# Stage one of a decoder layer in a written order, with constant products on TensorE, and the second pair's key sums two hooks later

## The chip, the cores and the metric

The kernel runs on one core of one Trainium2 chip. The metric is the device time of one execution in microseconds, the median over the runs. Engines are named as in the profile: PE (TensorE, products), DVE (VectorE), ACT (ScalarE), POOL (GpSimd) and SP (SyncE, which here only issues transfers).

## The reference

One decoder layer (DEPTH 1) on x of 1024 tokens by 1024 features. In the cut below `A`, `B` and `C` are the three head groups; the change touches the first product and the keys of group C.

```python
def rmsnorm(x, g):
    xf = x.astype(jnp.float32)
    y = xf * lax.rsqrt(jnp.mean(xf * xf, axis=-1, keepdims=True) + NORM_EPS)
    return (y * g.astype(jnp.float32)).astype(x.dtype)
...
    z = rmsnorm(h, norm_mix_g[l]) @ w_in[l]
    a_q, a_f, a_i, a_g, b_q, b_k, b_v, c_in = jnp.split(z, splits, axis=-1)
    o_a = hgrn2_mix(a_q, a_f, a_i, a_g, lbs[l], hgrn_gnorm_g[l])
    o_b = dilated_window_mix(b_q, b_k, b_v)
    o_c, v_first = rwkv7_mix(c_in, ...)
    h = h + jnp.concatenate([o_a, o_b, o_c], axis=-1) @ w_out[l]
    h = h + conv_glu_ffn(rmsnorm(h, norm_ffn_g[l]), ffn_up[l], ffn_conv_w[l], ffn_conv_b[l], ffn_down[l])
    gate = jax.nn.sigmoid(rmsnorm(h, norm_ple_g[l]) @ ple_gate[l])
    h = h + gate * (p[l] @ ple_proj[l])
return rmsnorm(h, final_norm_g)
...
# in rwkv7_mix: the keys are scaled to length one per head
    kk = heads(k * k_k)
    kk = kk / jnp.maximum(jnp.linalg.norm(kk, axis=-1, keepdims=True), 1e-12)
```

## The kernel before

The work lies with features on the 128 partitions and tokens along a row. x comes as eight blocks of 128 features by 1024 tokens, in two halves of 512 tokens (`hf` 0 and 1). A weight block (`w_in[j]`) has 128 output features by 1024 inputs.

Products are made from split operands: ACT casts a high part (`whi`, `xh`), DVE or POOL subtracts it for the low part (`wlo`, `xl`), and `mm3` issues three products of 128 by 512, hi by hi (L127), hi by lo (L129) and lo by hi (L131). A block of weights takes 8 steps `k` of three products for each half. Two low parts are made per block; `split_w` gives them to POOL and DVE in turn.

Stage one is `mix_norm`. It loads x, the first three weight blocks and the parameters `par`, and makes the products of blocks 0, 1 and 2 with x times the norm's weight `g`, but without the norm's factor per token. That factor is made beside it: ACT squares x (`ssq`), DVE adds the eight squares up (`acc`), PE sums them over the partitions (`factor_sums`, L164, out `ps_ss`), DVE and POOL make the reciprocal root (`rst`), and PE spreads it over the partitions (`factor`, L174), from where ACT copies it to `rstd`. The products' results (`dp`) are multiplied by `rstd` later.

Then `rwkv` works on two pairs of heads (p = 0, 1). `rwkv_prep` projects k, r and v (`mix_in`), each 8 steps with both halves, so 48 products. Functions hung in as hooks are called after a step of such a projection. The keys' path is: `key_norm` (ACT squares k into `kksq`), `key_sums` (PE sums them, L530, out `kks`; DVE and POOL make `kr`), `removal_keys` (PE spreads `kr`, L182, out `kkb`; DVE makes `kkn`, a, `ar` and `bhat`). From `bhat` ACT and POOL make blocks `bb`, and PE the scores `sc` (L608).

What sets the order: instructions of one engine run in the order in which they stand in its program. Where nothing is written, a scheduler chooses it from what is ready by its own reckoning. Inside `tc.manual_schedule(engines=...)` the engines named keep the order of the code; `rwkv_prep` has that for PE. SP, ACT and POOL each issue transfers on a queue of their own. The transfers of stage one all stand on SP's queue, except the last columns of `par` on POOL's.

Of the kernel before, what the change touches and what calls it, by code (L numbers as in the profile page):

```python
# [10 lines left out]
F32 = mybir.dt.float32  # L11
F32R = mybir.dt.float32r
U8 = mybir.dt.uint8
AF = mybir.ActivationFunctionType
# [4 lines left out]
P = 128  # L19
T = 1024  # L20
HT = 512
ND = 8
# [57 lines left out]
class Trunk:  # L80
# [244 lines left out]
    def mix_norm(self):  # L325


        nc = self.nc
        X = self.xall()
        self.X = X  # L330
        self.R = self.keep.tile([P, T], F32, name="rstd")
        g = self.par[:, PC_MIX:PC_MIX + ND]
        halves = [slice(hf * HT, (hf + 1) * HT) for hf in (0, 1)]
        self.ps0 = ExitStack()
        ps0 = self.ps0.enter_context(self.pool("ps0", space=PSUM))
        with self.tc.tile_pool(name="st", bufs=1) as sp:
            dummy = sp.tile([P, 1], F32, name="dummy")
            nc.scalar.activation(dummy, self.ones, AF.Square)
            nc.sync.dma_start(self.par[:, :PC_LORA], self.a["par"][:, :PC_LORA])
            xs = [[sp.tile([P, 2, HT], F32, name=f"x{k}_{hf}") for k in range(4)] for hf in (0, 1)]  # L340
            xT = self.a["xT"].rearrange("(a two) p t -> a p two t", two=2)
            raws = {}
            for hf, sl in enumerate(halves):
                raws[hf] = self.wpool.tile([P, 1024], F32, tag="wraw", name=self.nm("wraw"), bufs=2)
                nc.sync.dma_start(raws[hf], self.a["w_in"][hf])
                for k in range(4):
                    nc.sync.dma_start(xs[hf][k], xT[k][:, :, sl])
                if hf == 0:
                    raws[2] = sp.tile([P, 1024], F32, name="wraw2")
                    nc.sync.dma_start(raws[2], self.a["w_in"][2])  # L350
            self.load_params()
            w = {j: self.split_w(raws[j]) for j in (0, 1)}
            self.early = {j: self.dps.tile([P, T], F32, tag="dp", name=self.nm("dp")) for j in (0, 1)}
            self.early[2] = ps0.tile([P, T], F32, name="dp2")
            def split(hf, k, acc):
                x = xs[hf][k // 2][:, k % 2, :]
                hi, lo = X[k][0][hf], X[k][1][hf]
                nc.scalar.activation(hi, x, AF.Copy, scale=g[:, k:k + 1])  # L358
                nc.vector.scalar_tensor_tensor(lo, x, g[:, k:k + 1], hi.bitcast(F32), ALU.mult, ALU.subtract)  # L359
                t = sp.tile([P, HT], F32, tag="ssq", name=self.nm("ssq"), bufs=4) if k else acc  # L360
                nc.scalar.activation(t, x, AF.Square)
                if k:
                    nc.vector.tensor_tensor(acc, acc, t, ALU.add)

            def first_two(hf, k):
                for j in (0, 1):
                    self.mm3({hf: self.early[j][:, halves[hf]]}, w[j](k), X[k], k == 0, k == ND - 1, (hf,))

            def factor_sums(acc):
                return self.rstd_sums(acc, 1.0 / 1024, EPS, ps0.tile([P, 4], F32, tag="n", name=self.nm("ps_ss"), bufs=2))  # L370

            def factor(hf, r):
                pb = self.rstd_spread(r, ps0.tile([P, HT], F32, tag="n", name=self.nm("ps_ss"), bufs=2))
                nc.scalar.copy(self.R[:, halves[hf]], pb)

            acc = [sp.tile([P, HT], F32, tag="sacc", name=self.nm("acc"), bufs=2) for _ in halves]
# [108 lines left out]
    def rwkv_prep(self, p, tp, lt, d, j):  # L485

        tc, nc, par = self.tc, self.nc, self.par
# [7 lines left out]
        def c3(t):  # L495
            return t.rearrange("p (c i) -> p c i", i=64)
# [25 lines left out]
        def key_norm():  # L522
            sq = tr("kksq")
            nc.scalar.activation(sq, d["k"], AF.Square, scale=col(PC_KK))
            d["kksq"] = sq
# [1104 lines left out]
```

## Time and profile before

| what | value |
|---|---|
| median of 3 runs | 1525.62 us (1524.99 to 1525.76) |
| profiled execution | 1523.62 us, span 1521.6 us |
| instructions | 20022 |
| mean granted TensorE clock | 0.986 |
| ACT busy, POOL busy | 634.1 us, 434.8 us |
| HBM read, written | 120.12 MB, 46.40 MB |

The span goes from the first to the last instruction of the profiled execution, and the execution's time is 2.0 us longer. In the rows of the profile, a line `L127 PE MATMUL dp<-xh,whi` is an instruction of line 127 on PE that writes `dp` from `xh` and `whi`; behind it stands how many are merged in the row, and in brackets how long the engine had been idle and what ended that. In a row of windows there stand, for each engine, its busy microseconds and the number of instructions, then the granted PE clock, the share of time in which the 16 DMA engines were busy, and GB/s.

### The profile page before, as it was taken

How to read it: one execution, taken by the hardware profiler on the slowest of the kernel's cores; microseconds unless marked ns; L12 is line 12 of the kernel's file. 1: busy time of each engine (PE TensorE's matmuls, PEld its weight loads, DVE VectorE, ACT ScalarE, POOL GpSimd, SP SyncE). 2: the span in 40 equal slices, each digit the busy share in tenths (PEclk: the TensorE clock that was granted, in tenths of full speed). 3: DMA queues.
4: the chain of work that ended last, by engine and by line, in shares of the span. 5: the costliest groups of instructions: out<-in, count | busy, mean ns of one | idle time of the engine just before them, and what ended most of it. 6: DMA issues, size and time to landing. Idle time of an engine off the chain costs nothing.

```text
span 1521.6 us, 20022 instructions
## 1 busy us (share of the span) xinstructions
PE 1463.5 (96%) x7416; PEld 1208.0 (79%) x7416; DVE 1086.0 (71%) x1572; ACT 634.1 (42%) x1091; POOL 434.8 (29%) x361
## 2 busy tenths in 40 slices
PE   7999999999999999999999999999999999999995
PEld 5888887788887786778778888888888888888774
DVE  6667442665455678745888888888888799767684
ACT  6532322223324545425454444444444544455541
POOL 2334321415221132113124444444444000003330
PEclk9999999999999999999999999999999999999998
DMA  5224002133042121156333333333333873441352
GB/s 206 65 90 120 20 28 84 42 104 84 1 180 84 65 89 56 43 209 200 109 119 104 104 104 104 105 104 104 104 104 105 314 273 98 124 145 52 110 181 75
DMA packets 78705, 167.82 MB, mean 110 GB/s; under 512 B 19920, under 2 KB 20048, under 8 KB 78608
## 3 DMA queue, kind: packets, MB, share of 16 engines
q1 hardware_dynamic: 65120, 145.97, 29.6%
q10 hardware_dynamic: 12400, 16.52, 3.2%
q0 software_dynamic: 1088, 4.06, 0.8%
q8 instruction: 58, 0.95, 0.3%
q14 instruction: 39, 0.32, 0.1%
HBM read 120.12 MB, written 46.40 MB: 109 GB/s over the span
## 4 chain that ended last, share of the span: by engine, by line
PE 47%; issue 2%; DVE 2%; POOL 1%; ACT 1%; DMA 0%; POOLq 0%; DVEq 0%; ACTq 0%
PE bg L1185 15%; PE bv L1185 11%; PE bv L1476 7%; PE bg L1476 7%; PE dp L131 1%; PE dp L127 1%; PE dp L129 1%; PE bv L127 1%; PE bv L129 1%; PE bv L131 1%; PE bg L131 1%; PE bg L127 1%; PE bg L129 1%; POOL wlo L106 0%; DVE acc L194 0%
## 5 line engine op out<-in xcount | busy, mean ns | idle before, releaser
L127 PE MATMUL dp<-xh,whi 128*128 128x512 f32 x544 | 186.6, 401 | 8.4 <-ACT xh L358 8.4
L129 PE MATMUL dp<-xl,whi 128*128 128x512 f32 x544 | 184.3, 396 | 1.0 <-DVE xl L359 0.9
L131 PE MATMUL dp<-xh,wlo 128*128 128x512 f32 x544 | 182.9, 394 | 0.7 <-POOL wlo L106 0.5
L106 POOL TENSOR_TENSOR wlo<-wraw,whi 128x512 fp32r<-128x512 f32 x60 | 83.1, 1386 | 265.3 <-ACT whi L104 260.9
L106 POOL TENSOR_TENSOR wlo<-raw,whi 128x512 fp32r<-128x512 f32 x84 | 134.7, 1622 | 76.3 <-ACT whi L104 76.3
L104 ACT CAST whi<-wraw 128x512 fp32r<-128x512 f32 x120 | 73.1, 618 | 172.7 <-PE dp L129 129.8
L1185 PE MATMUL bg<-t,whi 128*128 128x512 f32 x352 | 133.2, 389 | 0.0
L127 PEld LDWEIGHTS dp<-xh,whi 128*128 128x128 f32 x544 | 101.5, 189 | 31.6 <-ACT xh L358 8.4
L129 PEld LDWEIGHTS dp<-xl,whi 128*128 128x128 f32 x544 | 102.2, 189 | 24.7 <-DVE xl L359 3.7
L131 PEld LDWEIGHTS dp<-xh,wlo 128*128 128x128 f32 x544 | 102.5, 189 | 22.1 <-POOL wlo L106 1.0
L106 POOL TENSOR_TENSOR wlo<-s,whi 128x512 fp32r<-128x512 f32 x44 | 64.2, 1460 | 172.3 <-ACT whi L104 172.3
L1476 PE MATMUL bg<-t,whi 128*128 128x512 f32 x308 | 95.2, 390 | 0.0
L1476 PE MATMUL bv<-t,whi 128*128 128x512 f32 x308 | 94.8, 389 | 0.0
L104 ACT CAST whi<-raw 128x512 fp32r<-128x512 f32 x88 | 52.7, 620 | 95.4 <-issue 48.6
L104 ACT CAST whi<-s 128x512 fp32r<-128x512 f32 x66 | 38.9, 620 | 122.0 <-PE bg L1185 113.3
L106 DVE TENSOR_TENSOR wlo<-wraw,whi 128x512 fp32r<-128x512 f32 x60 | 49.0, 816 | 43.4 <-ACT whi L104 40.1
L168 POOL TENSOR_TENSOR rst<-rst,mhalf 128x4 f32<-128x4 f32 x8 | 10.5, 1306 | 232.8 <-DVE rst L166 232.8
L1185 PEld LDWEIGHTS bg<-t,whi 128*128 128x128 f32 x352 | 66.0, 188 | 13.7
L1476 PEld LDWEIGHTS bv<-t,whi 128*128 128x128 f32 x308 | 57.8, 188 | 12.0
L1476 PEld LDWEIGHTS bg<-t,whi 128*128 128x128 f32 x308 | 57.7, 188 | 11.9
L1185 PE MATMUL bg<-t,wlo 128*128 128x512 f32 x176 | 67.2, 389 | 0.0
L1472 ACT CAST t<-t 128x512 fp32r<-128x512 f32 x77 | 47.8, 622 | 45.4 <-PE bv L1476 32.6
(403 smaller groups left out, 3686.2 us busy)
## 6 DMA issues: line engine op xcount, KB each, us to landing
raw<-in_ffn_up_dram SPq DMA_DIRECT2D x44, 512.0 KB, 3.7
wraw<-in_w_in_dram SPq DMA_DIRECT2D x30, 512.0 KB, 3.7
z<-zst SPq DMA_DIRECT2D x18, 512.0 KB, 3.0
gb<-ct SPq DMA_DIRECT2D x33, 256.0 KB, 2.0
t<-gb SPq DMA_DIRECT2D x33, 256.0 KB, 2.8
t<-gt SPq DMA_DIRECT2D x33, 256.0 KB, 2.7
zl<-z SPq DMA_DIRECT2D x16, 512.0 KB, 3.8
wraw<-in_ple_gate_dram SPq DMA_DIRECT2D x16, 512.0 KB, 3.6
```

Source lines behind the costliest of these rows:

```text
L104: nc.scalar.copy(hi, src)
L106: eng.tensor_tensor(lo, src, hi.bitcast(F32), ALU.subtract)
L127: nc.tensor.matmul(ps[hf], wh, xh[hf], start=first, stop=False)
L129: nc.tensor.matmul(ps[hf], wh, xl[hf], start=False, stop=False)
L131: nc.tensor.matmul(ps[hf], wl, xh[hf], start=False, stop=last)
L168: nc.gpsimd.tensor_tensor(r2, r, self.mhalf[:, :4], ALU.pow)
L1185: nc.tensor.matmul(ps, w[part == 2][:, s], X[k][part == 1], start=start and k == part == 0, stop=k == 3 and part == 2, skip_group_check=no ...
L1472: nc.scalar.copy(xh, x)
L1476: nc.tensor.matmul(ps[m], wt[part == 2][:, m * P:(m + 1) * P], (xh, xl)[part == 1], start=k == part == 0, stop=k == NK - 1 and part == 2)
```

## The change

In `mix_norm`, the first weight block comes in two halves and the first pair of x blocks in two transfers of one block each, the latter issued on ACT's queue (ACT issues the second one behind its table load). The three other pairs of x, then weight blocks 1 and 2, then the second half of x follow on SP's queue. PE's order in the whole stage is written out, and that of ACT and DVE up to the end of the first block on the first half of x. In that part block 0 alone is multiplied with x as it comes; both low parts of block 0 are made on DVE; the squares and sums are written behind it. PE gets 10 products of a constant tile `warm` (128 by 128) ahead of everything, and two more behind each of the first four steps, into a result that nobody reads. The first sums are called after step 1 of block 2 instead of 0, the spread after step 6 instead of 5.

In `rwkv_prep`, for the second pair alone, `key_sums` is called after step 7 of r's projection instead of 4, and `removal_keys` after step 2 of v's projection instead of 0.

```diff
-            raws = {}
+            raws = {j: self.wpool.tile([P, 1024], F32, tag="wraw", name=self.nm("wraw"), bufs=2) for j in (0, 1)}
+            raws[2] = sp.tile([P, 1024], F32, name="wraw2")
+            for c in (0, 1):
+                nc.scalar.dma_start(xs[0][0][:, c, :], self.a["xT"][c][:, :HT])
+                nc.sync.dma_start(raws[0][:, c * HT:(c + 1) * HT], self.a["w_in"][0][:, c * HT:(c + 1) * HT])
             for hf, sl in enumerate(halves):
-                raws[hf] = self.wpool.tile([P, 1024], F32, tag="wraw", name=self.nm("wraw"), bufs=2)
-                nc.sync.dma_start(raws[hf], self.a["w_in"][hf])
-                for k in range(4):
+                for k in range(1 - hf, 4):
                     nc.sync.dma_start(xs[hf][k], xT[k][:, :, sl])
                 if hf == 0:
-                    raws[2] = sp.tile([P, 1024], F32, name="wraw2")
-                    nc.sync.dma_start(raws[2], self.a["w_in"][2])
+                    for j in (1, 2):
+                        nc.sync.dma_start(raws[j], self.a["w_in"][j])
             self.load_params()
-            w = {j: self.split_w(raws[j]) for j in (0, 1)}
...
+            warm = sp.tile([P, 2 * P], F32, name="warm")
+            nc.vector.memset(warm, 1.0)
+            pw = ps0.tile([P, P], F32, tag="n", name="pwarm", bufs=2)
+
+            def idle_products(n):
+                for _ in range(n):
+                    nc.tensor.matmul(pw, warm[:, :P], warm[:, P:], start=True, stop=True)
...
-            for k in range(ND):
-                split(0, k, acc[0])
-                first_two(0, k)
-            w[2] = self.split_w(raws[2])
-            r = {}
-            self.dense({0: self.early[2][:, halves[0]]}, w[2], X, ND, halves=(0,),
-                       hooks={0: lambda: r.update(r=factor_sums(acc[0])), 5: lambda: factor(0, r["r"])})
-            for k in range(ND):
-                split(1, k, acc[1])
-            for k in range(ND):
-                first_two(1, k)
-                if k == 1:
-                    r = factor_sums(acc[1])
-                if k == 4:
-                    factor(1, r)
-            self.dense({1: self.early[2][:, halves[1]]}, w[2], X, ND, halves=(1,))
+            r, w, parts = {}, {}, []
+            w[0] = lambda k: tuple(t[:, (k % 4) * P:(k % 4 + 1) * P] for t in parts[k // 4])
+            with self.tc.manual_schedule(engines={E.PE}):
+                with self.tc.manual_schedule(engines={E.Activation, E.DVE}):
+                    idle_products(10)
+                    for k in range(ND):
+                        if k % 4 == 0:
+                            parts.append(self.split2(raws[0][:, k * P:k * P + HT], nc.vector))
+                        split(0, k)
+                        product(0, 0, k)
+                        idle_products(2 if k < 4 else 0)
+                w[1] = self.split_w(raws[1])
+                for k in range(ND):
+                    square(0, k, acc[0])
+                for k in range(ND):
+                    product(1, 0, k)
+                w[2] = self.split_w(raws[2])
+                self.dense({0: self.early[2][:, halves[0]]}, w[2], X, ND, halves=(0,),
+                           hooks={1: lambda: r.update(r=factor_sums(acc[0])), 6: lambda: factor(0, r["r"])})
+                for k in range(ND):
+                    split(1, k)
+                    square(1, k, acc[1])
+                for k in range(ND):
+                    for j in (0, 1):
+                        product(j, 1, k)
+                    if k == 1:
+                        r1 = factor_sums(acc[1])
+                    if k == 4:
+                        factor(1, r1)
+                self.dense({1: self.early[2][:, halves[1]]}, w[2], X, ND, halves=(1,))
...
-        r = self.mix_in(3 + 3 * p, 0 + p, "r", tr, {4: key_sums} if p else {2: decays, 4: key_sums})
+        r = self.mix_in(3 + 3 * p, 0 + p, "r", tr, {7: key_sums} if p else {2: decays, 4: key_sums})
...
-        v = self.mix_in(4 + 3 * p, 4 + p, "v", hooks={0: removal_keys})
+        v = self.mix_in(4 + 3 * p, 4 + p, "v", hooks={2 * p: removal_keys})
```

(`split` and `square` are the two halves of the old `split`; `product` is one block's part of the old `first_two`.)

What this does to the order, at three places. The numbers at the end of a name are running numbers: `x_0_131` to `x_0_134` are the four pairs of x of the first half, `xh_105` to `xh_119` (odd) and `xl_106` to `xl_120` (even) its eight steps; `wraw_139` is weight block 0.

First, DVE from its first low part on, before:

```order
L359 SCALAR_TENSOR_TENSOR xl_106<-x_0_131,par,xh_105 128x512
L359 SCALAR_TENSOR_TENSOR xl_108<-x_0_131,par,xh_107 128x512
L106 TENSOR_TENSOR wlo_162<-wraw_139,whi_160 128x512
L363 TENSOR_TENSOR acc_175<-acc_175,ssq_188 128x512
L359 SCALAR_TENSOR_TENSOR xl_110<-x_0_132,par,xh_109 128x512
L363 TENSOR_TENSOR acc_175<-acc_175,ssq_199 128x512
L359 SCALAR_TENSOR_TENSOR xl_112<-x_0_132,par,xh_111 128x512
L363 TENSOR_TENSOR acc_175<-acc_175,ssq_210 128x512
```

and after, from the second low part of x on:

```order
L368 SCALAR_TENSOR_TENSOR xl_108<-x_0_131,par,xh_107 128x512
L368 SCALAR_TENSOR_TENSOR xl_110<-x_0_132,par,xh_109 128x512
L368 SCALAR_TENSOR_TENSOR xl_112<-x_0_132,par,xh_111 128x512
L106 TENSOR_TENSOR wlo_214<-wraw_139,whi_212 128x512
L368 SCALAR_TENSOR_TENSOR xl_114<-x_0_133,par,xh_113 128x512
L368 SCALAR_TENSOR_TENSOR xl_116<-x_0_133,par,xh_115 128x512
L374 TENSOR_TENSOR acc_164<-acc_164,ssq_246 128x512
L368 SCALAR_TENSOR_TENSOR xl_118<-x_0_134,par,xh_117 128x512
L368 SCALAR_TENSOR_TENSOR xl_120<-x_0_134,par,xh_119 128x512
L106 TENSOR_TENSOR wlo_243<-wraw_140,whi_241 128x512
L374 TENSOR_TENSOR acc_164<-acc_164,ssq_249 128x512
```

All but one of the first half's sums (`acc`) stand behind its low parts now; five follow each other there, and then the second half's low parts and sums alternate as before.

Second, PE at the start of the program, before:

```order
L127 MATMUL dp_172<-xh_105,whi_156 128x512
L129 MATMUL dp_172<-xl_106,whi_156 128x512
L131 MATMUL dp_172<-xh_105,wlo_158 128x512
L127 MATMUL dp_172<-xh_107,whi_156 128x512
L129 MATMUL dp_172<-xl_108,whi_156 128x512
```

and after:

```order
L362 MATMUL pwarm<-warm 128x128 x10
L127 MATMUL dp_158<-xh_105,whi_180 128x512
L129 MATMUL dp_158<-xl_106,whi_180 128x512
L131 MATMUL dp_158<-xh_105,wlo_182 128x512
L362 MATMUL pwarm<-warm 128x128 x2
L127 MATMUL dp_158<-xh_107,whi_180 128x512
```

The constant products stand ahead of and between the first steps. Before, six steps of block 0 were followed by six of block 1 and then the last two of both; after, all eight of block 0 stand first, then all of block 1.

Third, PE in the second pair's r projection, before (`dp_2167` is r's result; `xh_113` and `xh_97` are step 4 of the two halves, `xh_115` and `xh_99` step 5):

```order
L131 MATMUL dp_2167<-xh_113,wlo_2165 128x512
L131 MATMUL dp_2167<-xh_97,wlo_2165 128x512
L530 MATMUL kks_2198<-few,kksq_2155 128x2 x8
L127 MATMUL dp_2167<-xh_115,whi_2163 128x512
L127 MATMUL dp_2167<-xh_99,whi_2163 128x512
```

and after (`dp_2196` is r's result now, `xh_119` and `xh_103` its last step; `dp_2273` is v's):

```order
L131 MATMUL dp_2196<-xh_119,wlo_2194 128x512
L131 MATMUL dp_2196<-xh_103,wlo_2194 128x512
L555 MATMUL kks_2245<-few,kksq_2184 128x2 x8
L127 MATMUL dp_2273<-xh_105,whi_2265 128x512
L127 MATMUL dp_2273<-xh_89,whi_2265 128x512
```

The sums moved from behind step 4 of r to the end of r. In the same way the 16 products of the spread (`kkb`) moved from behind v's first step to behind its third. On DVE `kr` now stands behind r's multiplication by `rstd`, and r's mixing and `ar` stand ahead of the two `kkn`.

More of the change, by code (lines that the diff above doesn't have):

```diff
@@ L341, in mix_norm, with split @@
             xT = self.a["xT"].rearrange("(a two) p t -> a p two t", two=2)
-            raws = {}
+            raws = {j: self.wpool.tile([P, 1024], F32, tag="wraw", name=self.nm("wraw"), bufs=2) for j in (0, 1)}
[3 more added lines that the diff above has]
+                nc.sync.dma_start(raws[0][:, c * HT:(c + 1) * HT], self.a["w_in"][0][:, c * HT:(c + 1) * HT])
             for hf, sl in enumerate(halves):
-                raws[hf] = self.wpool.tile([P, 1024], F32, tag="wraw", name=self.nm("wraw"), bufs=2)
-                nc.sync.dma_start(raws[hf], self.a["w_in"][hf])
-                for k in range(4):
+                for k in range(1 - hf, 4):
                     nc.sync.dma_start(xs[hf][k], xT[k][:, :, sl])
                 if hf == 0:
-                    raws[2] = sp.tile([P, 1024], F32, name="wraw2")
-                    nc.sync.dma_start(raws[2], self.a["w_in"][2])
+                    for j in (1, 2):
+                        nc.sync.dma_start(raws[j], self.a["w_in"][j])
             self.load_params()
-            w = {j: self.split_w(raws[j]) for j in (0, 1)}
             self.early = {j: self.dps.tile([P, T], F32, tag="dp", name=self.nm("dp")) for j in (0, 1)}
             self.early[2] = ps0.tile([P, T], F32, name="dp2")
-            def split(hf, k, acc):
+            warm = sp.tile([P, 2 * P], F32, name="warm")
[4 more added lines that the diff above has]
+                    nc.tensor.matmul(pw, warm[:, :P], warm[:, P:], start=True, stop=True)
+            def split(hf, k):
                 x = xs[hf][k // 2][:, k % 2, :]
@@ L359, in split, with square, product @@
                 nc.vector.scalar_tensor_tensor(lo, x, g[:, k:k + 1], hi.bitcast(F32), ALU.mult, ALU.subtract)
+            def square(hf, k, acc):
                 t = sp.tile([P, HT], F32, tag="ssq", name=self.nm("ssq"), bufs=4) if k else acc
-                nc.scalar.activation(t, x, AF.Square)
+                nc.scalar.activation(t, xs[hf][k // 2][:, k % 2, :], AF.Square)
                 if k:
                     nc.vector.tensor_tensor(acc, acc, t, ALU.add)
-            def first_two(hf, k):
-                for j in (0, 1):
-                    self.mm3({hf: self.early[j][:, halves[hf]]}, w[j](k), X[k], k == 0, k == ND - 1, (hf,))
+            def product(j, hf, k):
+                self.mm3({hf: self.early[j][:, halves[hf]]}, w[j](k), X[k], k == 0, k == ND - 1, (hf,))
             def factor_sums(acc):
@@ L374, in factor @@
                 nc.scalar.copy(self.R[:, halves[hf]], pb)
+            E = mybir.EngineType
             acc = [sp.tile([P, HT], F32, tag="sacc", name=self.nm("acc"), bufs=2) for _ in halves]
-            for k in range(ND):
-                split(0, k, acc[0])
-                first_two(0, k)
-            w[2] = self.split_w(raws[2])
-            r = {}
-            self.dense({0: self.early[2][:, halves[0]]}, w[2], X, ND, halves=(0,),
-                       hooks={0: lambda: r.update(r=factor_sums(acc[0])), 5: lambda: factor(0, r["r"])})
```

## The prediction

> **What bounds the kernel now.** I read the page's first two sections, then who waited for whom on PE, then the timelines of the two places that the change touches, then the transfers.
>
> ```profile
> PE 1463.5 (96%) x7416; PEld 1208.0 (79%) x7416; DVE 1086.0 (71%) x1572; ACT 634.1 (42%) x1091; POOL 434.8 (29%) x361
> ...
> PE   7999999999999999999999999999999999999995
> ```
>
> PE is busy 96% of the span, and nine tenths or more in every slice but the first and the last. So the kernel is worth its PE time plus PE's waits; anything that shortens PE's own path at one place shortens the whole, as long as the other engines there hang on PE. Of PE's waits these two lie where the change is:
>
> ```profile
> PE dp L127 <- ACT xh L358: 8.4, 1, 8.4
> ...
> PE kks L530 <- ACT kksq L524: 2.5, 1, 2.5
> ```
>
> Stage one on PE (start, time, instruction; the step between two starts is the price):
>
> ```profile
> 8.41 0.80 PE L127 MATMUL dp<-xh,whi 128*128 128x512 f32 x1 [8.41 <-ACT xh L358]
> ...
> 10.22 0.63 PE L127 MATMUL dp<-xh,whi 128*128 128x512 f32 x1
> 10.65 0.63 PE L129 MATMUL dp<-xl,whi 128*128 128x512 f32 x1
> ...
> 20.15 0.39 PE L127 MATMUL dp<-xh,whi 128*128 128x512 f32 x1
> 20.37 0.39 PE L129 MATMUL dp<-xl,whi 128*128 128x512 f32 x1
> ...
> 24.91 0.95 PE L164 MATMUL ps_ss<-few,acc 128*128 128x1 f32 x8
> ...
> 33.78 0.95 PE L164 MATMUL ps_ss<-few,acc 128*128 128x1 f32 x8
> ...
> 48.76 0.62 PE L127 MATMUL dp<-xh,whi 128*128 128x512 f32 x2
> ```
>
> The first products step by 0.43 us, later ones by 0.227 (0.22 to 0.23 a row): PE begins at half speed. The stage ends at 48.76. Its 144 products at 0.227 are 32.7 us; with some 2.3 us of sums and spreads that makes 35.0, so of 48.76 about 8.4 us are the start and 5.3 us slow or waiting products. VectorE has no such slack:
>
> ```profile
> 9.53 0.75 DVE L359 SCALAR_TENSOR_TENSOR xl<-x,par,xh 128x512 fp32r<-128x512 f32 x1 [0.38 <-ACT xh L358]
> ...
> 11.40 0.74 DVE L359 SCALAR_TENSOR_TENSOR xl<-x,par,xh 128x512 fp32r<-128x512 f32 x1
> 12.06 0.68 DVE L363 TENSOR_TENSOR acc<-acc,ssq 128x512 f32<-128x512 f32 x1
> 12.66 0.74 DVE L359 SCALAR_TENSOR_TENSOR xl<-x,par,xh 128x512 fp32r<-128x512 f32 x1
> ...
> 16.46 1.77 DVE L359 SCALAR_TENSOR_TENSOR xl<-x,par,xh 128x512 fp32r<-128x512 f32 x1
> ...
> 31.25 0.68 DVE L363 TENSOR_TENSOR acc<-acc,ssq 128x512 f32<-128x512 f32 x1
> 34.77 0.16 DVE L166 TENSOR_SCALAR rst<-ps_ss 128x4 f32<-128x4 f32 x1 [2.84 <-PE ps_ss L164]
> ```
>
> From 9.53 to 31.93 it has no gap: an xl steps 0.66, an acc sum 0.60. PE takes acc's last sum at 33.78, 1.85 us after it is there. That is all the room PE has to come earlier before it waits for VectorE.
>
> **The change, part by part.** First, the transfers:
>
> ```profile
> 2.00:4.00 2.00, 0.00 (x0) 0.00 (x0) 0.72 (x5) 0.43 (x3) 0.21 (x2) 1.00 0.96 286
> ...
> 10.00:15.00 5.00, 4.33 (x12) 2.32 (x12) 5.00 (x9) 5.00 (x10) 0.00 (x0) 1.00 1.04 404
> ```
>
> ```profile
> 2.12 0.47 SPq L347 DMA_DIRECT2D x<-in_xT_dram  x1
> ```
>
> ```profile
> x<-in_xT_dram SPq DMA_DIRECT2D x1, 512.0 KB, 6.8
> ```
>
> ```profile
> 5.44 1.14 ACT L104 CAST whi<-wraw 128x512 fp32r<-128x512 f32 x2 [2.14 <-DMA wraw<-in_w_in_dram]
> 7.64 0.72 ACT L358 ACTIVATE xh<-x,par 128x512 fp32r<-128x512 f32 x1 [1.06 <-DMA x<-in_xT_dram]
> ```
>
> Windows end with the DMA share and GB/s: the engines are full from 2 us on, at 286 and later 404 GB/s. The first product now needs half of the first weight block and one x tile, 512 KB less than before. At those rates that is 1.3 to 1.8 us, so it starts near 6.8 instead of 8.41. The second x pair (issued 2.12, landed 6.8 later, at 8.9) has the same bytes ahead of it in both kernels. If the second queue fills the slow stretch up to 404 GB/s, 0.24 MB go earlier, or 0.6 us. So it lands at 8.3 to 8.9; I take 8.6.
>
> Second, VectorE. From the second pair on it has work without a gap again: its xl can start 0.8 us after the landing (ACT's 0.72 and two hand-overs), at 9.4. Before, from the same xl (11.40) to the last acc sum (31.93) was 20.5 us, for 14 xl, 13 sums and 2 wlo. In the new order the first acc sum and a wlo that stood ahead of that point (or ran on POOL) come behind it: 1.2 us more, 21.7. The two collisions with a POOL wlo (16.46 shows one, 1.77 for 0.74) stay two. acc is complete at 9.4 + 21.7 = 31.1, with bounds 30.8 and 31.4.
>
> Third, PE. Its last products of the first block wait for the last xl of the half. From 9.4 VectorE has five xl, a wlo and a sum, then the eighth xl's 0.75: 14.7, and with two more products 15.1. The second block adds 24 x 0.227 = 5.4, the third's two steps 1.4; from first sums to second sums it was 33.78 - 24.91 = 8.9, now one step (0.7) less. So PE arrives at the second sums at 15.1 + 5.4 + 1.4 + 8.2 = 30.1, and waits about 1.0 us for acc at 31.1. From the sums on nothing is different: 14.98 us to the end of the stage, now 46.1. Gain 33.78 - 31.1 = 2.7 us, bounds 2.4 to 3.1. Half a microsecond more or less in the first products costs nothing, because VectorE decides.
>
> The 18 constant products: a product is two passes, and a pass that loads 128 columns and streams little costs 1.81/16 = 0.113 us (the key sums below), at half speed twice that. Ten cost 2.3 to 4.5 us from about 1.3, done by 3.6 to 5.8, ahead of the first real product; two behind each of four steps (0.5 us) lie where PE waits for x anyway. They cost nothing; without that cover they would cost 4.1 warm. What they bring, full speed before 12 us, is also behind VectorE, so it is no term of the sum. The squares that move behind the splits are in VectorE's count; on ACT a pair of xh and square steps 1.13 us, VectorE's xl and sum 1.26, so ACT stays ahead:
>
> ```profile
> 9.92 0.71 ACT L358 ACTIVATE xh<-x,par 128x512 fp32r<-128x512 f32 x1
> ...
> 11.05 0.71 ACT L358 ACTIVATE xh<-x,par 128x512 fp32r<-128x512 f32 x1
> ```
>
> POOL loses one wlo. The third and fourth weight blocks' loads hang on PE freeing slots, and move with it.
>
> Fourth, the second pair's key sums:
>
> ```profile
> 272.83 0.61 PE L131 MATMUL dp<-xh,wlo 128*128 128x512 f32 x2
> 275.96 1.95 PE L530 MATMUL kks<-few,kksq 128*128 128x2 f32 x16 [2.52 <-ACT kksq L524]
> 277.77 0.79 PE L127 MATMUL dp<-xh,whi 128*128 128x512 f32 x2
> ...
> 282.20 0.62 PE L127 MATMUL dp<-xh,whi 128*128 128x512 f32 x2
> ...
> 285.02 1.97 PE L182 MATMUL kkb<-cst,kr 128*64 128x128 f32 x32
> ...
> 299.30 0.94 PE L608 MATMUL sc<-ar,bb 128*128 128x128 f32 x7
> ```
>
> ```profile
> 274.85:278.26 3.41, 2.29 (x18) 2.25 (x19) 0.87 (x2) 1.57 (x2) 0.06 (x1) 1.00 0.00 0
> 278.30:281.60 3.30, 3.30 (x9) 2.56 (x8) 0.00 (x0) 0.00 (x0) 2.80 (x1) 0.50 0.00 0
> ...
> 59.50:62.80 3.30, 3.30 (x16) 2.69 (x16) 2.12 (x4) 1.13 (x2) 2.96 (x2) 1.00 0.00 0
> ```
>
> PE waits 2.52 us for kksq, and then, with a granted clock of 0.50, issues the twelve products from 277.77 to 282.20 in 4.43 us instead of 12 x 0.227 + 0.1 = 2.8: another 1.6. At 59.50, just behind the first pair's key sums, which had no wait, the clock is 1.00; so the wait is what takes the speed away. The price of the hook's place is 2.5 + 1.6 = 4.1.
>
> ```profile
> 274.76 1.15 ACT L524 ACTIVATE kksq<-k,par 128x1024 f32<-128x1024 f32 x1 [1.35 <-DVE k L456]
> ```
>
> ```profile
> 278.20 2.90 POOL L534 TENSOR_TENSOR kr<-kr,mhalf 128x16 f32<-128x16 f32 x1 [9.93 <-DVE kr L532]
> ```
>
> ```profile
> 292.07 1.22 DVE L550 TENSOR_TENSOR bhat<-a,ig 128x1024 f32<-128x1024 f32 x1
> ```
>
> Now three steps (18 products, 4.1 us) stand ahead: PE reaches the sums at 273.4 + 4.1 = 277.5, and kksq is there at 275.9. Sums until 279.3, three steps of v until 283.4, then kkb. On the way kr: VectorE by 279.6 (behind r's scaling), POOL 2.90, so 282.6: 0.8 us early. What is late next is bhat: kkb is done at 285.3 instead of 286.9, but r's mixing and ar no longer stand between; bhat ends near 290 against 293.3 before. The scores (299.30 before) come at 295.2, and had about 6 us after bhat; now 5. No new wait. Gain 4.1, bounds 2.5 (the clock loss stays) and 4.1.
>
> Sum: 2.7 + 4.1 = 6.8 us. The profiled execution took 1523.62 (span 1521.6 and 2.0 around it), so 1516.8; the median of the runs lies 2.0 above it at 1525.62, so **1518.8** as a median. 0.2%, about what a measurement of this kernel can tell, is 3.05 us.
>
> A rule against a term: the Trainium skill, "TensorE: Matmul & The Clock Gate", section "Why this matters for your kernels", says that clock drops mid-kernel come from PE gaps of more than about 3 us. By it 2.52 us of waiting would not drop the clock, and the half speed would stay with the sums; the sum would be 2.7 + 2.5. The trace has 0.50 behind the wait with sums and 1.00 behind sums without a wait, so I keep 4.1 and take the other as a rival.
>
> **Rivals.** (a) *Half speed stays, or returns.* Either low work in the sums alone brings it, against the row at 59.50; or the new wait ahead of stage one's second sums (1.0 us and 0.95 of sums, idle or light work for PE) grows past 1.5 us and drops the clock there. Either way 1.6 back: 1520.4. For it: the wait is new, and its size is a difference of two long sums. (b) *The second x piece is late.* ACT issues it only behind its table load, near 2.7, when SP has 2 MB queued. If it lands with what SP issued by then, near 10, ACT and VectorE start late: xl at 10.7, one xl more, acc at 33.1, gain 0.7 instead of 2.7: 1520.8. Against it: POOL's parameters, on a queue of their own beside SP's full one, landed 5.0 us after their issue.
>
> ```profile
> par<-in_par_dram POOLq DMA_DIRECT2D x1, 256.0 KB, 5.0
> ```
>
> (c) *VectorE is freer than I say*, because its collisions with POOL (1.0 us each) fall elsewhere: then acc is there at 29.1 and PE decides, at 29.8 with the second x pair early: gain 4.0: 1517.5. (d) *Slower.* The constant products hold PE. Real work then starts at 1.3 + 20p for a warm price p, since ten run at half speed, and the first block ends 5.4 + 8p later; all behind it is PE's chain of 15.0 to the second sums. It eats the 4.1 too, and is slower by 0.2%, from 6.7 + 28p + 15.0 = 33.8 + 4.1 + 3.05, that is p = 0.69 us; with p = 0.75 it gives 1530. The rows say 0.23. (e) *The order does nothing in stage one*, since VectorE was the bound all along and starts no earlier: 4.1 alone, 1521.5.
>
> **How the numbers follow.** Forecast 1518.8 (1518.0 to 1519.6 with the bounds of stage one) 0.50; (a) 0.17; (b) 0.09; (c) 0.13; (d) 0.03; (e) 0.08. From (c) less the 0.8 us that the runs spread, and half a microsecond more, to (e) with the same half, 1516.0 to 1522.0 leaves out (d) and the tails. Faster by over 0.2% (under 1522.6) are all but (d) and the worst of (a), (b) and (e) together: 0.88; same 0.09; slower 0.03.
>
> **What the profile after would show.** First real product at 6 to 7.5 us with a step of 0.227 by 9; VectorE without a gap from about 9.4; a short PE wait for acc ahead of the second sums at 31; the stage's end at 46.1; no wait of kks on kksq, and a clock of 1.00 behind the sums. It is wrong if the second x tile's xh starts after 8, if PE's wait for acc is over 1.5 us, if kkb waits for kr, or if a wait of the scores takes the place of the one removed.

## The result and the profile after

The kernel after took 1520.91 us (median of 6 runs, 1516.91 to 1522.63) against 1525.57 us before: ratio 0.9970, 95% interval 0.9959 to 0.9980, or 4.7 us (3.0 to 6.3). Timed once more beside e7 and e8 (the run e5 below) it was 0.9966 (0.9957 to 0.9975). The forecast was 1518.8, with a range of 1516.0 to 1522.0. The profiled execution took 1520.86, 2.8 us less than the one before; the sum had asked for 6.8. First, who waited for whom on PE:

```profile
PE swq L1063 <- DMA zl<-z: 4.0, 1, 4.0
...
PE swq L1063 <- DVE zst L438: 1.4, 1, 1.4
PE dp L127 <- ACT xh L367: 1.4, 1, 1.4
...
PE ps_ss L164 <- DVE acc L374: 0.9, 1, 0.9
```

The wait of kks is gone, and of the 8.4 us at the start 1.4 are left between the constant products and the first real one. New are 0.9 us for acc, which was forecast, and two longer waits of swq far behind the change, which were not. (swq are the score products of group B's attention. `z` goes from the tile `zst` to HBM and comes back from there as `zl`.) The same two before:

```profile
PE swq L1038 <- DMA zl<-z: 1.9, 1, 1.9
PE swq L1038 <- DVE zst L413: 1.1, 1, 1.1
```

Stage one on PE, then on VectorE (timelines):

```profile
1.25 4.64 PE L362 MATMUL pwarm<-warm 128*128 128x128 f32 x20 [1.25 <-DVE few L266]
7.25 0.50 PE L127 MATMUL dp<-xh,whi 128*128 128x512 f32 x1 [1.36 <-ACT xh L367]
...
23.22 0.95 PE L164 MATMUL ps_ss<-few,acc 128*128 128x1 f32 x8
...
32.47 1.02 PE L164 MATMUL ps_ss<-few,acc 128*128 128x1 f32 x8 [0.88 <-DVE acc L374]
...
47.55 0.62 PE L127 MATMUL dp<-xh,whi 128*128 128x512 f32 x2
```

```profile
9.68 1.42 DVE L368 SCALAR_TENSOR_TENSOR xl<-x,par,xh 128x512 fp32r<-128x512 f32 x2 [0.34 <-ACT xh L367]
...
14.86 1.79 DVE L106 TENSOR_TENSOR wlo<-wraw,whi 128x512 fp32r<-128x512 f32 x1
16.57 3.87 DVE L374 TENSOR_TENSOR acc<-acc,ssq 128x512 f32<-128x512 f32 x5
20.36 1.78 DVE L106 TENSOR_TENSOR wlo<-wraw,whi 128x512 fp32r<-128x512 f32 x1
...
31.65 0.68 DVE L374 TENSOR_TENSOR acc<-acc,ssq 128x512 f32<-128x512 f32 x1
```

The stage ends at 47.55 instead of 48.76: 1.2 us gained, not 2.7. VectorE completes acc at 32.33, 0.4 us later than before (31.93); PE, which had taken that sum at 33.78, now stands there in time and waits. What was gained is PE's room and nothing else. The second pair, on PE and in the windows of the clock:

```profile
276.17 1.84 PE L555 MATMUL kks<-few,kksq 128*128 128x2 f32 x16
277.87 0.72 PE L127 MATMUL dp<-xh,whi 128*128 128x512 f32 x2
...
282.18 1.97 PE L182 MATMUL kkb<-cst,kr 128*64 128x128 f32 x32
...
293.73 1.95 PE L633 MATMUL sc<-ar,bb 128*128 128x128 f32 x16
```

```profile
275.75:279.17 3.42, 3.42 (x25) 3.11 (x24) 1.95 (x4) 1.74 (x2) 2.14 (x2) 1.00 0.12 14
279.20:282.60 3.40, 3.40 (x22) 2.59 (x22) 2.15 (x2) 0.00 (x0) 2.00 (x1) 1.00 0.37 139
```

No wait, full clock behind the sums, no new wait of kkb or sc. Laid beside the trace of before, the same PE instruction stands 1.21 us earlier behind stage one and 5.57 us earlier at the scores (293.73 against 299.30). So the pair gave 4.4. At 452 the lead is 5.3, behind the wait for zl at 529 it is 3.2, and a half-clock stretch there of 6.83 us (3.41 before) leaves about 2. So some 3 us were given back by 540, at a place that the change does not touch.

### The profile page after: what moved, and what is told of

Same layout as the page of the kernel before. It is cut to its first block, busy times and chain, and to the rows that moved or that the text cites. A ratio compares the mean times of both kernels' runs of the same rounds, so it can differ in the third digit from the quotient of the medians.

```text
span 1519.0 us, 20098 instructions
## 1 busy us (share of the span) xinstructions
PE 1468.0 (97%) x7452; PEld 1213.5 (80%) x7452; DVE 1087.5 (72%) x1574; ACT 634.8 (42%) x1091; POOL 431.6 (28%) x360
```

## The experiments

"Lead at 290" is how much earlier than in the trace of before the same PE instruction stands behind the second pair's sums: it is free of what happens later. It hangs on how stage one began in that execution (5.6 in the kernel after, 4.8 in e5, which is the same code), but the pair's part of it does not: in all ten traces with the second pair's hooks moved and single sums the lead grows by 4.36 to 4.37 us from ahead of the sums to behind them. Ratios are to the kernel before, timed beside the run.

### The second pair alone (e1)

```diff
-        r = self.mix_in(3 + 3 * p, 0 + p, "r", tr, {4: key_sums} if p else {2: decays, 4: key_sums})
+        r = self.mix_in(3 + 3 * p, 0 + p, "r", tr, {7: key_sums} if p else {2: decays, 4: key_sums})
-        v = self.mix_in(4 + 3 * p, 4 + p, "v", hooks={0: removal_keys})
+        v = self.mix_in(4 + 3 * p, 4 + p, "v", hooks={2 * p: removal_keys})
```

> The kernel before with the second pair's two hooks moved (key sums after step 7 of r, spread after step 2 of v), and stage one as it was. Theory: the hooks alone give what the kernel after showed there: the 2.5 us wait of kks on kksq is gone, the granted clock behind the sums is 1.00 (it was 0.50 for 3.4 us), and the scores come 4.1 us earlier than in the kernel before at the same point, so about 1521.4 as a median. Rival one (the half speed belongs to the sums, not to the wait): the wait goes but the step of the products behind the sums stays 0.37 us for 3.4 us; 2.5 us, 1523. Rival two (the longer wait of swq for zl near 530, 4.0 us instead of 1.95 in the kernel after, is brought by the earlier second pair): that wait is about 4 us here too, and of the 4.1 us only 1 to 2 reach the end, 1524.

Measured: 0.9960 (0.9945 to 0.9974) of the time before; in time the pair alone is not less than the whole change (0.9959 to 0.9980). Stage one stands 0.2 us late, the lead at 290 is 4.2: again 4.4 from the pair. In the window behind the sums the clock is 1.00 (third number from the end), and swq waited 1.9 us for zl. Both rivals fall.

```profile
279.30:282.60 3.30, 3.30 (x16) 2.70 (x17) 2.50 (x3) 0.91 (x1) 2.93 (x2) 1.00 0.49 159
```

### Stage one alone (e2)

The same two lines turned back in the kernel after.

> The kernel after with the two hooks put back (key sums after step 4 of r, spread after step 0 of v), so stage one's part alone. Theory: stage one ends at 47.5 (48.76 before), 1.2 us gained; at the second pair the 2.5 us wait and the half clock are back; median about 1524.3. Rival one (most of the stage's predicted 2.7 us is there, and the profiled execution of the kernel after had a bad start): stage end 46.1, median 1522.9. Rival two (the wait for zl near 530 grows because of stage one): about 4 us there, and a median at or above the one before, 1525.5 to 1527.

Measured: 1.0010 (0.9998 to 1.0021): no gain. In its trace stage one's 1.2 us are there, but the old wait is back with a half-clock stretch of 6.83 us, and swq at 453 waited 2.1 us for zst instead of 1.1 (below). The theory's time did not come. The time is that of rival two, but not by its cause: the wait for zl was 1.9 us, not 4. So 1.2 us are less than what else changed. The windows at the old wait:

```profile
271.08:274.49 3.41, 1.18 (x6) 0.64 (x4) 1.28 (x1) 2.03 (x2) 0.00 (x0) 1.00 0.00 0
274.49:281.32 6.83, 6.54 (x23) 5.89 (x24) 0.87 (x2) 0.74 (x2) 2.68 (x1) 0.50 0.00 0
```

The window ahead of the drop holds 1.18 us of full products (a share of 0.35) and 2.23 us of waiting, but none of the sums, which start at 274.78. So here the wait alone was enough.

### The wait filled (e6)

In the kernel before:

```diff
+            if p:
+                pw = self.mxp.tile([P, HT], F32, tag="mx", name="pwarm")
+                for _ in range(10):
+                    nc.tensor.matmul(pw[:, :P], self.ident, self.ident, start=True, stop=True)
             for tb in range(8):
                 nc.tensor.matmul(pss[:, 2 * tb:2 * tb + 2], d["kksq"][:, tb * P:(tb + 1) * P], self.bone2, ...)
```

> The kernel before with the second pair's key sums where they were (after step 4 of r), and ten products of the constant identity, 128 by 128, into a tile that nobody reads, on PE ahead of them: the wait for kksq stays, but is filled (10 x 0.23 = 2.3 us of the 2.5). Theory (it is PE's idling that takes the speed away): kks starts at 275.96 as before, and the granted clock behind the sums is 1.00, the twelve products behind them take 2.8 us instead of 4.4; 1.6 us gained at 290, median 1.6 us under the one before. Rival (the sums with their two streamed columns bring the half speed, idle or not): clock 0.50 for 3.4 us behind them as before, gain 0 at 290.

PE's idle time fell to 0.29 us, and the clock dropped all the same (PE's timeline, then the windows):

```profile
273.39 2.39 PE L532 MATMUL pwarm<-cst 128*128 128x128 f32 x20
276.07 1.95 PE L534 MATMUL kks<-few,kksq 128*128 128x2 f32 x16 [0.29 <-ACT kksq L524]
...
279.40 1.05 PE L127 MATMUL dp<-xh,whi 128*128 128x512 f32 x2
```

```profile
275.84:279.25 3.41, 3.18 (x22) 2.98 (x23) 0.87 (x2) 0.69 (x2) 0.94 (x1) 1.00 0.00 0
279.25:282.66 3.41, 3.41 (x10) 2.63 (x9) 0.00 (x0) 0.00 (x0) 1.96 (x1) 0.50 0.00 0
```

Lead at 290: none (0.1 late); ratio 0.9994 (0.9985 to 1.0003). The rival holds. In the 3.41 us ahead of the drop PE is "busy" 3.18 us, but only from 277.88 on with full products: 1.37 of 3.41, a share of 0.40.

### The sums twice (e9)

In the kernel after without constant products:

```diff
-            for tb in range(8):
+            for tb in list(range(8)) * (1 + p):
```

> The kernel after without the constant products, and with the second pair's eight key sums issued twice in a row (the second time over the first): no wait, but 3.5 us instead of 1.8 in which PE streams two columns at a time. Theory (the clock follows the share of a 3.41 us window in which PE streams; behind windows of 0.14 and 0.40 it fell, behind 0.49 and 0.50 it did not): the sums now fill half a window or more in every phase, so the granted clock behind them is 0.50 for at least 3.41 us; the products behind them step 0.43 us, and at 290 the kernel is 1.75 + 1.5 us behind the one with single sums. Rival (only idle time counts, and small sums count as work): clock 1.00, 1.75 us behind.

On PE's timeline there is no wait at all, and yet the clock falls, for two windows:

```profile
276.42 4.14 PE L552 MATMUL kks<-few,kksq 128*128 128x2 f32 x32
280.42 1.20 PE L127 MATMUL dp<-xh,whi 128*128 128x512 f32 x2
```

```profile
275.93:279.34 3.41, 3.41 (x30) 3.29 (x29) 1.51 (x2) 1.73 (x2) 1.27 (x1) 1.00 0.13 13
279.34:286.17 6.83, 6.83 (x21) 5.57 (x21) 2.59 (x3) 0.00 (x0) 2.90 (x1) 0.50 0.18 70
```

The lead at 290 is 0.4 us, 5.2 less than with single sums (e3), of which 0.2 are stage one's (expected 3.3: the second window was not foreseen); ratio 0.9990 (0.9981 to 1.0000). The window ahead of the drop holds 0.49 us of wide products (512 columns), a share of 0.14. The theory holds: what counts is how much of a window of 3.41 us PE spends streaming wide products, and sums of two columns count nearly as idle time. At half speed a share counts for less: e9's first half-speed window had 0.68 of wide products and another one followed, e2's second had 0.91 and none did.

### No constant products (e3), old transfers as well (e8)

```diff
-            nc.vector.memset(warm, 1.0)
-                    idle_products(10)
-                        idle_products(2 if k < 4 else 0)
```

> The kernel after without the constant products and their memset. Theory (VectorE decides stage one): the first products step 0.43 us until about 11 us, but the second sums still start within 0.2 us of 32.47, PE's 0.88 us wait ahead of them only shrinks, stage one ends at 47.5, and the median stays at 1520.9 within 1 us. Rival (PE's full speed from 6 us on is what the stage lives on): first block's end later by 1.5 us or more, stage end 48.2 to 49, median 1521.7 to 1522.5.

e8 takes these lines out too, and issues the transfers as before:

```diff
-            for c in (0, 1):
-                nc.scalar.dma_start(xs[0][0][:, c, :], self.a["xT"][c][:, :HT])
-                nc.sync.dma_start(raws[0][:, c * HT:(c + 1) * HT], self.a["w_in"][0][:, c * HT:(c + 1) * HT])
             for hf, sl in enumerate(halves):
-                for k in range(1 - hf, 4):
+                nc.sync.dma_start(raws[hf], self.a["w_in"][hf])
+                for k in range(4):
...
```

> The kernel after without the constant products, and with the transfers as in the kernel before: the whole first weight block, then x in pairs, all on SP's queue. So of stage one's change only the written order is left. Theory (the transfers brought nothing, because the second x pair lands at 8.9 in both and VectorE decides from there): first product at 8.5 instead of 7.4, VectorE's xl of the second pair within 0.4 us of 9.9, second sums within 0.4 us of 32.5, stage end 47.5 to 47.9. Rival (the early first x block is what the order lives on): VectorE carries the 1.1 us on, stage end 48.5 or later, no better than before.

| kernel | first product | second x pair landed | first, second sums on PE | lead at 45 us |
|---|---|---|---|---|
| before | 8.41 | 8.87 | 24.91, 33.78 | 0 |
| after | 7.25 | 8.89 | 23.22, 32.47 | 1.21 |
| e3, no constants | 7.42 | 9.14 | 24.07, 32.49 | 1.19 |
| e8, old transfers too | 8.49 | 8.95 | 24.59, 32.79 | 0.99 |

The theory holds in both: with the products at half speed until 11.71 the second sums start 0.02 us later. Of the 1.21 us the written order gives 0.99. The 0.20 of the transfers and the 0.02 of the constants are no more than two executions differ by: e9, whose stage one is that of e3, has 0.97 there. But in time both are better than the kernel after looked: e3 0.9954 (0.9940 to 0.9968), e8 0.9956 (0.9943 to 0.9968), about 7 us. That was not expected, since their leads at 290 (5.6 and 5.3) are no better than the 5.6 of the kernel after, and it led to e5, e10 and e11.

### Sums called later (e4)

```diff
-                    if k == 1:
+                    if k == 2:
                         r1 = factor_sums(acc[1])
-                    if k == 4:
+                    if k == 5:
                         factor(1, r1)
```

> The kernel after with the sums of the second half called one step later (after step 2 instead of 1), and their spread after step 5 instead of 4. Theory (VectorE ends its adding 0.9 us after PE arrives, and PE has other products to do meanwhile): the 0.88 us wait ahead of the second sums is gone, stage one ends at 46.7 instead of 47.55, median 0.9 us lower, 1520.0. Rival one (something behind it waits instead: the spread for the reciprocal root, or the products of the second half for their xl): a wait of about the same size elsewhere in stage one, end at 47.5. Rival two: what is gained here is lost at a later wait for a transfer.

The wait went, but the stage still ended at 47.43, ratio 0.9972 (0.9962 to 0.9982). It does not tell the theories apart, because PE itself was late: the second x pair landed at 9.39 in this execution, and the clock that the constants had brought at 6.27 was lost again at 9.69, so that a pair of constant products took 1.06 us (0.61 in the kernel after) and PE reached the second sums at 33.81.

### Low parts on VectorE (e7), and the best version (e12)

In e3:

```diff
-                w[1] = self.split_w(raws[1])
+                w[1] = split_v(raws[1])
...
-                w[2] = self.split_w(raws[2])
+                w[2] = split_v(raws[2])
```

(`split_v` makes both low parts of a block on VectorE.)

> The kernel after without the constant products, and with the low parts of weight blocks 1 and 2 all on VectorE: POOL makes none in stage one. Theory (VectorE's 22.65 us from the second x pair to the last acc sum held two collisions with POOL of 1.1 us each, and PE waited 1.1 us for a low part that took POOL 2.9 us): VectorE has two more low parts of 0.6 us and loses 2.2 us, so it is done at 31.4 to 31.6 instead of 32.35; first sums at 23.0 instead of 24.07, second sums at 31.5, stage end 46.6 instead of 47.57; 1.0 us under the version without constants. Rival one (VectorE has no room): two more low parts in its program push xl back, PE waits for xl or wlo, the second sums stay at 32.5 or later, end 47.6 to 48.2.

VectorE's timeline of e7, from the second x pair to the last sum:

```profile
9.77 1.42 DVE L367 SCALAR_TENSOR_TENSOR xl<-x,par,xh 128x512 fp32r<-128x512 f32 x2 [0.34 <-ACT xh L366]
...
14.96 1.28 DVE L106 TENSOR_TENSOR wlo<-wraw,whi 128x512 fp32r<-128x512 f32 x2
16.17 2.28 DVE L373 TENSOR_TENSOR acc<-acc,ssq 128x512 f32<-128x512 f32 x3
...
30.62 0.68 DVE L373 TENSOR_TENSOR acc<-acc,ssq 128x512 f32<-128x512 f32 x1
```

VectorE does two low parts more and is done at 31.30, in 21.53 us instead of the 22.43 of e3; lead at 45 us 2.22 (e3: 1.19). The theory holds: the stage hangs on VectorE, and about 2 us of VectorE's time were its collisions with POOL (22.43 - 21.53 + two low parts of 0.60 = 2.1; in e3's rows a sum of 1.57 instead of 0.69 and a low part of 1.78 instead of 0.68). Ratio 0.9953 (0.9941 to 0.9966). e12 adds the later sums of e4:

> The version without constant products and with all low parts of blocks 1 and 2 on VectorE, with the second half's sums called one step later as well (after step 2, their spread after step 5). It had PE waiting 0.54 us for acc, which is done at 31.3. Theory: no wait, second sums at 32.3, stage end 46.0 instead of 46.5, 0.5 us more at 290 (7.2 us ahead of the kernel before there), median 7.5 to 8.5 us under it. Rival (as where the sums were called later before: something else takes the wait's place): stage end 46.5 again.

Second sums at 32.18 without a wait, lead 2.96 at 45 us and 7.3 at 290, ratio 0.9948 (0.9935 to 0.9962): 7.9 us faster than before, the lowest ratio of all, though its interval overlaps those of e3, e7 and e8. The step from e7 at 45 us is 0.74, of which 0.25 came from x landing earlier (8.74 after 8.99); the rest is the 0.5 expected.

### Where the later microseconds went (e5, e10, e11)

e5 is the kernel after, unchanged.

> The kernel after, unchanged, timed beside the three others of this set, since its version without constant products was 3.8 us below its median on another chip, with the same instructions in the same order from 47.6 us on. Theory (the later differences, at 450 and 530 us, are one execution's luck): the runs spread over 1516 to 1523 us as the version without the constants does, the median lies within 1.5 us of 1519, and the wait of swq for zl near 530 is 2 or 4 us. Rival (the constant products cost something later): a median of 1520.5 or more, and again 3.5 to 4 us of waiting for zl.

e10 has the constants at the front alone:

```diff
-                    idle_products(10)
+                    idle_products(13)
-                        idle_products(2 if k < 4 else 0)
```

> The kernel after with 13 constant products ahead of everything and none between the steps. They end at 7.2 us (13 x 0.46), just ahead of the first real product. In stage one: no idle gap, so the granted clock stays 1.00 from 6 us on in every phase; VectorE decides, stage end 47.4 to 47.6. Theory for the later loss (52 more PE instructions move PE's own instruction fetches 5.9 us ahead, into the store of z near 434 and the loads of zl near 521): a fetch within z's transfer, z lands 5.7 us or more after its issue, and swq waits 1.4 to 2.0 us for zst instead of 1.1. Rival (luck of the execution): z lands within 5.3 us, swq waits 1.1, and the median is that of the version without constants, 7 us under the kernel before.

e11 has more of them:

```diff
                 self.dense({1: self.early[2][:, halves[1]]}, w[2], X, ND, halves=(1,))
+                idle_products(14)
```

> The kernel after with 14 more constant products at the end of stage one: 14 x 0.23 = 3.2 us of PE, and 56 more PE instructions, which move PE's instruction fetches 6.3 us ahead of where the kernel after has them, relative to the work. Theory (fetches that fall into the z and zl transfers lengthen them): the fetches fall 3 to 4 us ahead of the store of z and of the loads of zl, z lands 5.0 to 5.3 us after its issue (5.8 in the kernel after), swq waits 1.1 us for zst (1.4) and 1.7 to 2.1 for zl (4.0); of the 3.2 us at least 1.5 come back by 540. Rival (luck, or another effect of the constants): waits as in the kernel after, and 3.2 us slower than it.

e5: 1519.44 us (1516.91 to 1521.51), waits of 2.4 us for zl and 1.9 for zst, lead at 290 4.8. Between theory and rival: the median is the theory's, the wait for zl is not fixed, the one for zst is long again. Here the constants did not even bring the clock: products stepped at half speed until 14.09, x landed at 9.32, and the stage's lead was 0.4 us.

What differs is PE's own instruction fetch. The transfer records list it as a queue of its own, 58 fetches of 16 KB, one for about 257 PE instructions (14,904 in 58). The 18 constants are 72 instructions ahead of all others, so each fetch comes earlier in the work: the one in question at 436.5 us, in e3 at 443.1. In the kernel after one falls into the store of z (issued at 434.06), where e3 has none; both are the transfer view of the store's span:

```profile
q8 instruction: 1, 0.02, 1.3%
...
z<-zst SPq DMA_DIRECT2D x1, 512.0 KB, 5.8
```

```profile
z<-zst SPq DMA_DIRECT2D x1, 512.0 KB, 5.0
```

Over all 14 profiles the split is clean: with a fetch inside (after, e2, e4, e5) that store took 5.8, 6.6, 6.0 and 6.3 us, without one (the ten others) 4.9 to 5.3; swq then waited for zst 1.4 to 2.1 us against 1.1 to 1.35. (Four loads of zl stand behind the store on the same queue, and VectorE works on them ahead of zst: the first landed at 441.11 in the kernel after and at 440.23 in e3.) In e11, with the most constants of all, the fetch came 3.9 us ahead of the store, as expected, and the store took

```profile
z<-zst SPq DMA_DIRECT2D x1, 512.0 KB, 5.3
```

The waits there were 1.3 us for zst (1.1 expected) and 2.0 for zl, where the rival has 1.4 and 4.0. So for the length of the store it is where the fetch falls that counts, not the constants as such; the waits for zst differ little (1.3 against 1.4). (e11's time says less, 0.9999, 0.9990 to 1.0008: its 14 products held up the next stage by a further wait of 2.5 us and another half-clock stretch.) In e10 the fetch came at 439.4, just behind the landing, and the store took 4.9: expected otherwise, but by the same rule. The fetch fell into the loads of zl instead: the second landed 2.33 us behind the first (1.28 in e3), and the wait for zst was 1.34. Stage one of e10 came out as expected (full clock from 4.83 on, end at 47.53); ratio 0.9962 (0.9949 to 0.9975).

Open stays the wait for zl near 529, 4.0 us in the kernel after and 3.7 in e4. In both a fetch came 0.2 us behind the load's issue, and the load took 7.3 and 7.0 us. But e2 has a fetch at the same distance, and e10 one at 0.6, with loads of 5.2 and 5.3. Also open is how much the constants cost in all: e3 and e4, timed together, are 0.9940 to 0.9968 and 0.9962 to 0.9982, which touch; so are e8 and e5, 0.9943 to 0.9968 and 0.9957 to 0.9975.

## Why the prediction was right, and where it was not

**The pair: right in size, half wrong in its reason.** Gain 4.4 for a forecast of 4.1, in all ten traces with the hooks moved. kks, kkb and sc stand where they were put: 277.5, 283.4 and 295.2 less stage one's 1.2, against 276.17, 282.18 and 293.73. But "the wait is what takes the speed away" is half of it. With e6 and e9 the clock drops without the wait's idle time, and in e2 it dropped with the wait and none of the sums in the window. Wait and sums together left wide products a share of 0.14 of the window (0.49 us of 274.85 to 278.26); filled, 0.40; as moved, 0.50 (all but 276.17 to 277.87 of the window shown above), and the clock stays. In the new wait and sums of stage one, which rival (a) feared, the share was 0.48 (29.99 to 33.41), and it stayed as well. The first pair's sums, on which the argument rested, are the same case as the moved ones. The Trainium skill ("TensorE: Matmul & The Clock Gate", "Why this matters for your kernels") asks for a PE gap of over 3 us. The traces differ: 0.50 behind 0.29 us of idling, and behind none. Its section "What's actually happening" there says that the clock is set by activity in a free-running window of 3413 ns; with that the traces agree: every half-speed stretch between 15 and 1500 us lasts 3.41 or 6.83 us, and its place shifts from one execution to the next.

**Stage one: the term was mis-sized, 1.2 for 2.7.** "VectorE decides" is right (e3, e7), and so is the start of the first product (7.25). Three sizes failed.
- "0.24 MB go earlier, or 0.6 us": the second x pair landed at 8.89, in other executions of the new transfers at 8.74 to 9.39, with the old ones at 8.87 to 9.07. The second queue brought nothing; VectorE began at 9.68, not 9.4. (The second x piece was issued at 1.27, not 2.7, so rival (b) had no ground.)
- "21.7": it took 22.65. Five sums in a row step 3.79 / 5 = 0.76 us, where the forecast took the 0.60 of sums that alternate with xl: 0.8 of the 0.95.
- "The two collisions stay two at 1.0": right in number, 2.2 us together (1.79 + 1.78 less two low parts of 0.68). It was a price that the change could have taken away, as e7 does. The Trainium skill ("SBUF — State Buffer", "SBUF: two separate sides") says that VectorE and GpSimd hold a shared port in turn for a whole instruction. The traces agree: a low part of 0.68 us took 1.79 while POOL made one, and ended 0.55 us behind POOL's end (14.34 + 1.76 against 14.86 + 1.79).

PE's own arrival was mis-sized too: it reached the second sums at 31.59, not 30.1. With acc at the forecast 31.1 the gain would have been 2.2 at most.

**"They cost nothing"** was right for the constants' place in stage one, where full speed brought 0.02 us. It was wrong in what was counted: not their time, but their 72 instructions, which moved a fetch by 6.6 us into a store 430 us later. What that cost is small in the profiled execution, 0.3 us of lead there (0.3 to 1.0 in the four traces with a fetch in the store, 0 to 0.25 in the others); the larger loss, at zl, is not traced to it. Their gain was also not sure: of six traces with constants at the front the clock stayed up in two (after, e10), was lost again for 3.41 us in two (e2, e4), and came only at 10.5 and 14.1 in two (e11, e5).

**The sum.** 2.7 + 4.1 became 1.2 + 4.4 = 5.6 at 290, and 3 us of it were given back later in the profiled execution. The median lies 2.1 us over the forecast, near rivals (a), (b) and (e), but for none of their reasons: the clock neither stayed down behind the sums nor fell ahead of stage one's second sums, and stage one gave something. What the forecast had no term for is that waits elsewhere move by 1 to 2 us: beside the trace of before, 11 of the other 13 lost 0.2 to 3.4 us between 290 and 540, and e12 and e3 gained 0.2 and 0.4. So that the median lies inside the range is in part luck.

## What to carry to other kernels

Count filler instructions on PE by their number as well as their time: they move every later instruction fetch, and the trace's transfer view shows where one falls into a transfer that somebody waits for (here 0.3 to 1.0 us). For the clock, add up over 3.41 us how long PE streams wide products; narrow sums count with the gaps, so put them between full products (0.48 and 0.50 held, 0.40 and, in e11, 0.44 did not). Before reordering around an engine that decides a stage, look in its rows for instructions that take 1.8 us instead of 0.7: taking POOL's part off it gave as much (1.0 us) as the whole new order.

## What the runs showed of the hardware that was not expected

- The clock falls without any gap: 0.50 for 6.83 us behind 4.0 us of two-column sums (e9), and behind a share of 0.40 with 0.29 us of idling (e6); shares of 0.50 kept 1.00 (after, e3, e4, e5, e10, e11, e12).
- With constant products from 1.25 us on, full clock came at 4.8 to 6.3 us where they filled 0.89 or more of a window of 3.41 us (e10, e2, after, e4), and at 10.5 and 14.1 us where they filled 0.76 at most (e11, e5); without them at 11.7 to 14.9.
- Each half-clock window costs up to 1.7 us of PE, and not every execution has the same ones: near 450 us five of the 14 traces have one, near 748 nine. That may be part of the 6 us over which 20 runs of the kernel before spread (1520.47 to 1526.62).
- A 16 KB instruction fetch inside a 512 KB store went with 0.5 to 1.7 us more for the store.
- VectorE's sums that follow each other on one accumulator step 0.79 us, before other work 0.60 (0.76 on average over the five).
